# A hybrid decoder block: cross attention's scores bound behind the next projection, its turned weights in other rows, a bank for the sums of squares, and copies of the down projection's last banks

## The chip, the cores and the metric

The kernel runs on one core of a Trainium2 chip. The metric is device time in microseconds, as the median of several runs. One execution was also recorded by the hardware profiler; its span, from the first to the last instruction, is what the profile's positions refer to.

The engines are called as in the profile: PE (TensorE, matmuls; PEld is its loading of the stationary operand), DVE (VectorE), ACT (ScalarE), POOL (GpSimd) and SP (SyncE). Here POOL does almost nothing but issue DMAs, and SP nothing else.

## The reference

One decoder layer over 512 tokens of width 2048, in float32:

```
h = RMSNorm(x); one projection h @ w_in feeds
    8 sparse-attention heads (compressed, selected and window branches, gated) and
    4 gated-linear-attention heads
x = x + concat(heads) @ w_out
cq = RMSNorm(RMSNorm(x) @ w_cq, per head) / sqrt(128)       # 4 heads of 128
s  = cq . ck  over 256 memory tokens;  p = softmax(s)
x  = x + (p @ cv) @ w_co
g, u = split(RMSNorm(x) @ w_gu)                              # 2 x 5632
out = x + (silu(g) * u) @ w_down
```

All of it is computed by both versions of the kernel.

## The kernel before

**Arithmetic.** Every float32 operand of a large product is split in a high part (ACT, a cast) and a low part (DVE, the difference), both in a reduced-precision format, and a product is three matmuls: high by high, high by low, low by high (`mm3`). A weight column block costs one DMA on SP's queue into a staging buffer (tag "w", four of them, later "raw"), one cast on ACT and one subtraction on DVE, and its pair of parts lives in "wh"/"wl" (later "qh"/"ql").

**Banks.** The eight PSUM banks (512 columns each) are handed out by tag: "mm" three, "s" two, "t" two, "o" one. A tile of a tag waits until one of that tag's banks has been read for the last time by its former owner.

**Order.** The source states the order of the work, and a planner that estimates durations may let an instruction that is not ready in its estimate be passed by later ones of its engine; `high_priority(offset)` lets some (weight loads above all) go earlier. `behind(i)` makes every instruction written inside it follow `i` on `i`'s engine. Once planned, each engine runs its list strictly in that order. The side work of the projections is written as generators: `flows.tick()` is called after every six matmuls of a projection (two k tiles), and `yield n` lets n ticks pass.

**Projections and sparse-attention heads** (from about 380 to 715 us of the profile). `project` accumulates 16 k tiles into an "mm" bank: 48 matmuls. A head starts when its projection is done: it splits q, squares it, has DVE turn the squares and sum them in part (`partial_sums`), and four ticks later `total_sums` (L338) finishes the sum over the head's 128 features with one small matmul, which the profile shows as two of 16 columns ("s<-qs,every"). From the result come the factors with which ACT writes the distance biases and takes exponentials, so scores can be computed before it, but not read. Eight score blocks per head go through the two "s" banks. The first head (number 0) starts ahead of `natural(w_vsw, ...)` (L1109), a product in the other orientation that makes the values of the selected and window branches; its four accumulators take the tags "mm", "mm", "o", "mm" until `natural_end` has read them. Its side work, ticks included, runs in that product.

**Cross attention** (from about 877 to 940 us). Four heads, `cross_head` (L1198): after the head's projection, ACT and DVE split q into two Q rows; two ticks later (one in the last head) come the scores, four blocks of 128 tokens by 256 memory tokens, two per "s" bank, 12 matmuls of 256 columns; then the sums' matmul (tag "t"), the softmax on DVE and ACT in two halves "e" of 256 tokens, and the turning of the weights so that memory tokens lie on partitions. Heads 2 and 3 turn them on PE. Heads 0 and 1 turn them with DVE inside 32 x 32 blocks, write them to DRAM with POOL's DMAs and read them back in place: one tile z of tag "w" for both halves of the memory tokens, two transposes of 512 columns, four writes (one per 32 partitions, L1250), two readings into "st" rows (L1253). Ten ticks later the rows are split into "PH"/"PL" and multiplied with the values into bank "o". `spare` rows of the tags "rs" and "q1" are used only later, for squares; one of the two "q1" rows holds a piece of x.

**Down projection** (the last 480 us). It runs in four steps over 22 k-pairs, seven products in place of eight, each into a set of four banks: set 0 is "mm", "o", "t", "t", set 1 is "s", "s", "mm", "mm". After a step its banks are added to or subtracted from parts of the result ("res", `gather`). At the end of step 2 (the third) set 0 was copied by ACT into a row H (L1832), from which twelve additions were spread over step 3, one per k-pair from the fourth on (L1819); set 1 was gathered straight from its banks by eight DVE additions (`pending`, L1762) before step 3 wants them. In that step a k-pair's weights are loaded, added on DVE (L1708), cast by ACT and subtracted by DVE into "qh"/"ql" (L204).

Of the kernel before, what the change touches and what calls it, by code (L numbers as in the profile page):

```python
# [10 lines left out]
F32 = mybir.dt.float32  # L11
# [9 lines left out]
MEM = 256  # L21
# [42 lines left out]
def hybrid_block(ctx: ExitStack, tc: tile.TileContext, x_t, mem_t, sv, cmat, umask, w_a, w_r67, w_v, w_vg, w_v3,  # L64
# [14 lines left out]
    def sb(shape, tag, bufs, dt=F32):  # L79
        return (pool_b if tag in LATE else pool).tile(shape, dt, name=tag, tag=tag, bufs=bufs)  # L80
# [23 lines left out]
    def row(tag, dt=F32):  # L104
        return sb([128, 512], tag, BUFS[tag], dt)
# [89 lines left out]
    def behind(*instructions):  # L195
        stack = ExitStack()
        for i in instructions:
            stack.enter_context(tc.issue_after(i.ins))
        return stack
# [54 lines left out]
    def mm3(ps, lhs, rhs, start, stop, again=False):  # L254
        mm(ps, lhs[0], rhs[0], start=start, stop=False, skip_group_check=again)
        mm(ps, lhs[0], rhs[1], start=False, stop=False, skip_group_check=again)
        mm(ps, lhs[1], rhs[0], start=False, stop=stop, skip_group_check=again)

    def part(pair, a, n):
        return pair[0][:, a:a + n], pair[1][:, a:a + n]  # L260

    def view(t, at, *dims):
        return bass.AP(tensor=t.tensor, offset=t.offset + at, ap=[list(t.ap[0])] + [list(d) for d in dims])
# [74 lines left out]
    def total_sums(dst, part, tag):  # L338
        ps = bank(tag)
        mm(ps[:, :16], every32, part, start=True, stop=True)  # L340
        p4 = part.rearrange("p (i g) -> p i g", g=4)
        V.tensor_mul(p4, ps[:, :16].rearrange("p (i g) -> p i g", g=4),
                     own32[:, None, :].to_broadcast([128, NT, 4]))
        V.reduce_sum(dst, p4, axis=AX.X)
# [581 lines left out]
    def nsa_head(h, ps):  # L926
# [7 lines left out]
        sc, sl, neg, part_, m3 = qt[:, 0:4], qt[:, 4:8], qt[:, 8:12], qt[:, 12:28], qt[:, 28:29]  # L934
        partial_sums(part_, sq, row("n"))
        yield W_SUM + 1
        total_sums(neg, part_, "s")
        V.tensor_mul(neg, neg, rc2)
        inv_rms(sc, neg, 128, sl)
        V.tensor_mul(sc, sc, rc)  # L940
# [257 lines left out]
    def cross_head(h, ps):  # L1198
        q = row("Q", F32R), row("Q", F32R)
        sq = row("n")  # L1200
        S.activation(sq, ps, AF.Square)
        split(*q, ps, g_cq)
        cf = triple("cf")
        sc, tmp, v = cf[:, 0], cf[:, 1], cf[:, 2]
        if h < 3:
            part_ = small("qs", 2)[:, :16]
            partial_sums(part_, sq, row("n"))
        yield 1 if h == 3 else 2
        if h == 3:
            pn = bank("t")  # L1210
            for i in range(NT):
                mm(pn[:, i:i + 1], sq[:, 128 * i:128 * i + 128], one, start=True, stop=True)
        scores = [bank("s") for _ in range(2)]
        for a in range(2):
            for i in range(2):
                mm3(scores[a][:, MEM * i:MEM * i + MEM], part(q, 128 * (2 * a + i), 128), part(ckp, MEM * h, MEM),
                    start=True, stop=True)
        if h < 3:
            total_sums(v, part_, "t")
        V.tensor_mul(v, v if h < 3 else pn[:, :NT], rc[1])  # L1220
        inv_rms(sc, v, 128, tmp)
        V.tensor_mul(sc, sc, rc[0])
        sm, mn = triple("sm"), triple("mn")
        halves = []
        for a in range(2):
            s = scores[a]
            p = row("e")
            two = slice(2 * a, 2 * a + 2)
            V.tensor_reduce(mn[:, 0, two], s.rearrange("p (i n) -> p i n", i=2), axis=AX.X, op=OP.max, negate=True)
            V.tensor_mul(mn[:, 0, two], mn[:, 0, two], sc[:, two])  # L1230
            for i in range(2):
                j = 2 * a + i
                S.activation(p[:, MEM * i:MEM * i + MEM], s[:, MEM * i:MEM * i + MEM], AF.Exp,
                             bias=mn[:, 0, j:j + 1], scale=sc[:, j:j + 1], accum_out=sm[:, 0, j:j + 1])
            V.reciprocal(mn[:, 1, two], sm[:, 0, two])
            for i in range(2):
                j = 2 * a + i
                pi = p[:, MEM * i:MEM * i + MEM]
                V.tensor_scalar(pi, pi, mn[:, 1, j:j + 1], None, op0=OP.mult)
            halves.append(p)  # L1240
        rows = []
        if h < 2:
            z = sb([128, 1024], "w", 4)
            for a in range(2):
                V.transpose(view(z, 64 * a, (32, 2), (128, 8), (1, 32)), halves[a])
            d = dram.tile([128, 1024], F32, name="crossp", tag="crossp", bufs=2)
            dv = d.rearrange("(c s) (b a x) -> s b c a x", s=32, b=2, a=4)
            zv = z.rearrange("p (b c x) -> p b c x", b=2, c=4)
            for a in range(4):
                G.dma_start(dv[:, :, :, a], zv[32 * a:32 * a + 32])  # L1250
            for b in range(2):
                rows.append(row("st"))
                G.dma_start(rows[b], d[:, 512 * b:512 * b + 512])  # L1253
        yield 6 if h == 3 else 10 if h < 2 else 4
        pts = []
        for b in range(2):
            pt = sb([128, 1280], ("PH", "PL")[b], PTB, F32R)
            pts.append((pt[:, :512], pt[:, 512:1024]))
            if rows:
                split(*[view(t, 0, (32, 4), (128, 4), (1, 32)) for t in pts[b]],  # L1260
                      rows[b].rearrange("p (a i x) -> p a i x", a=4, i=NT))
                continue
            tp = bank("t")
            for i in range(NT):
                c = MEM * (i % 2) + 128 * b
                PE.transpose(tp[:, 128 * i:128 * i + 128], halves[i // 2][:, c:c + 128], ident)
            split(*pts[b], tp)
        yield 2 if h == 3 else 1
        o = bank("o")
        for b in range(2):  # L1270
            mm3(o, part(cvp[b], 128 * h, 128), pts[b], start=b == 0, stop=b == 1)
        pair = row(OC[h], F32R), row(OC[h], F32R)
        split(*pair, o)
        oc.append(pair)
# [509 lines left out]
    for step, plan in enumerate(STEPS):  # L1784
        rs_ = range(len(plan))
        for kp in range(NK):
            if step or kp % 2 == 0:
                load_w(step, kp)

            if kp == 1:  # L1790
                for s in pending:
                    gather_all(s)
                if step == 0:
                    banks[0] = banks[1]
                elif step == 2:
                    banks[1] = [bank(t) for t in SETS[1]]
                else:
                    banks = [[bank(t) for t in SETS[r]] for r in rs_]
            if kp in (1, NK - 1):
                for r in rs_ if kp == 1 else reversed(rs_):  # L1800
                    for x in range(4):
                        for k in (kp - 1, kp):
                            down_product(step, r, k, (x,))
                        if step == 3 and kp == NK - 1:
                            gather(ADD, *((0, 0), (1, 0))[r], banks[r], x, True)
            elif 1 < kp < NK - 2:
                for r in rs_:
                    down_product(step, r, kp, range(4))
            if kp in ROWS[step]:
                load_rows(*ROWS[step][kp])  # L1810
            if kp in SUMS[step]:
                add_rows(*SUMS[step][kp])
            if step == 0 and kp == 3:
                last_turn = turn(hs, NB - 1)
            if kp >= 3 or step:
                for go in last_turn.get(NK * step + kp, ()):
                    go()
            move_h(step, kp)
            if step == 3 and kp > 2 and spread:  # L1819
                with behind(*last_split):  # L1820
                    gather(*spread.pop(0))
        if step == 0:
            pending = [(COPY, 0, 1, banks[0])]
            res[0, 1] = new_res(0, 1)
        elif step == 1:
            pending = [(COPY, 0, 0, banks[0]), (COPY, 1, 1, banks[1]), (ADD, 0, 1, banks[1])]
            for a in range(2):
                res[a, a] = new_res(a, a)
        elif step == 2:
            u = quarters(sb2("H"))  # L1830
            for x in range(4):
                S.copy(u[x], banks[0][x])  # L1832
            pending = [(SUB, 1, 1, banks[1]), (ADD, 1, 0, banks[1])]
            spread = [(*p, x, last) for *p, last in ((SUB, 1, 1, u, True), (SUB, 0, 1, u, True), (ADD, 1, 0, u, False))
                      for x in range(4)]


_OUT = (4, 128, 2048)
# [120 lines left out]
```

## Time and profile before

| | |
|---|---|
| three runs, median (lowest to highest) | 2243.55 us (2241.65 to 2248.02) |
| the profiled execution | 2241.54 us |
| its span | 2239.8 us |
| PE busy | 2229.3 us, 10404 matmuls |
| DVE busy | 1709.5 us |
| ACT busy | 1159.6 us |
| POOL busy | 299.7 us |

In the timeline a row is: start, duration, engine, line of the code, operation, destination<-sources, shape, count of merged instructions, and in brackets the idle time just ahead of it with what ended it. Since almost every matmul is written in one helper (L110), they are told apart by their tiles. In the rows of windows the columns are: window, its length, then busy time and (number of instructions) of PE, PEld, DVE, ACT and POOL, the granted clock of PE, the share of DMA time and GB/s. A row of waits says who waited for whom: total, number, longest. In rows by line "a/b/c" are the shortest, median and longest in ns. Matmuls overlap, so their spacing, not their duration, is what one costs. PE counts as busy while matmuls are in its pipeline; a short wait is seen as a gap between two starts.

### The profile page before, as it was taken

Reading aid. Unit: us, or ns where it says so; the run is one execution under the profiler, and the core shown is the slowest. Engines: PE = TensorE matmul, PEld = TensorE weight load, DVE = VectorE, ACT = ScalarE, POOL = GpSimd, SP = SyncE. Lnnn points to the kernel's source line nnn. Section 1 sums busy time; section 2 is a strip of 40 time slices with the busy share of each in tenths; the row PEclk is TensorE's granted clock in tenths of the full one; section 3 lists DMA queues with packets and bytes.
Section 4 is the critical chain, followed back from the end, with each engine's and each line's share of the span. In section 5 each row is a group of like instructions: output and inputs, shape, how many; then the busy total and the mean of one; then the engine's idle time right before and its main releaser. Section 6 shows DMA issues by size and latency. Waiting matters only on the chain.

```text
span 2239.8 us, 29015 instructions
## 1 busy us (share of the span) xinstructions
PE 2229.3 (100%) x10404; PEld 1851.8 (83%) x10404; DVE 1709.5 (76%) x2653; ACT 1159.6 (52%) x1715; POOL 299.7 (13%) x453
## 2 busy tenths in 40 slices
PE   9999999999999999999999999999999999999999
PEld 8898888888887888888888888888888888888887
DVE  7648986667878336788889888988888886766786
ACT  7534564556777324575455445544554554454443
POOL 0122221122221220120011101110110011001000
PEclk9999999999999999999999999999999999999999
DMA  8588778965563983595456546554664477768684
GB/s 305 179 220 201 190 188 223 248 172 170 151 169 112 250 229 95 162 265 201 148 184 197 173 150 195 189 170 154 198 201 142 150 281 261 268 241 281 250 278 163
DMA packets 130784, 448.23 MB, mean 200 GB/s; under 512 B 16240, under 2 KB 17520, under 8 KB 127696
## 3 DMA queue, kind: packets, MB, share of 16 engines
q1 hardware_dynamic: 81040, 304.71, 39.8%
q0 software_dynamic: 47152, 137.39, 24.7%
q10 hardware_dynamic: 2448, 4.28, 0.5%
q8 instruction: 81, 1.33, 0.2%
q14 instruction: 63, 0.52, 0.1%
HBM read 401.10 MB, written 107.09 MB: 227 GB/s over the span
## 4 chain that ended last, share of the span: by engine, by line
PE 96%; DVE 2%; DMA 1%; ACT 1%; issue 1%; SPq 0%; DVEq 0%; POOLq 0%; ACTq 0%
PE mm L110 52%; PE t L110 18%; PE s L110 14%; PE o L110 11%; PE t L1072 1%; DMA raw<-gu 0%; DMA raw<-td 0%; DMA PH<-w_ck 0%; DMA ss<-q 0%; DMA ss<-KV 0%; DVE ql L204 0%; DVE e L741 0%; DVE P L1017 0%; DVE wl L204 0%; ACT wh L204 0%
## 5 line engine op out<-in xcount | busy, mean ns | idle before, releaser
L204 ACT CAST qh<-raw 128x1024 fp32r<-128x1024 f32 (+1 forms) x494 | 478.5, 976 | 468.2 <-PE o L110 128.0
L204 DVE TENSOR_TENSOR ql<-raw,qh 128x1024 fp32r<-128x1024 f32 (+1 forms) x494 | 550.6, 1124 | 106.1 <-PE mm L110 40.1
L110 PE MATMUL mm<-X,wh 128*128 128x512 f32 x1664 | 524.4, 394 | 0.0
L110 PEld LDWEIGHTS mm<-X,wh 128*128 128x128 f32 x1664 | 306.4, 188 | 59.1 <-issue 0.8
L110 PE MATMUL t<-qh,PB 128*128 128x512 f32 x968 | 333.0, 389 | 0.0
L110 PE MATMUL mm<-X,wl 128*128 128x512 f32 x832 | 325.6, 392 | 0.5 <-DVE wl L204 0.5
L110 PE MATMUL mm<-qh,PB 128*128 128x512 f32 x868 | 309.1, 389 | 0.1
L204 DVE TENSOR_TENSOR wl<-w,wh 128x1024 fp32r<-128x1024 f32 (+2 forms) x172 | 205.5, 1200 | 130.8 <-ACT wh L204 127.9
L204 ACT CAST wh<-w 128x1024 fp32r<-128x1024 f32 (+2 forms) x172 | 176.8, 1033 | 232.9 <-PE mm L110 151.8
L110 PE MATMUL s<-qh,PB 128*128 128x512 f32 x672 | 231.0, 389 | 0.0
L110 PE MATMUL mm<-qh,PA 128*128 128x512 f32 x640 | 220.0, 389 | 0.0
L110 PEld LDWEIGHTS t<-qh,PB 128*128 128x128 f32 x968 | 181.7, 188 | 37.9
L110 PEld LDWEIGHTS mm<-qh,PB 128*128 128x128 f32 x868 | 163.0, 188 | 34.2 <-ACT qh L204 0.7
L110 PE MATMUL t<-ql,PB 128*128 128x512 f32 x484 | 188.3, 389 | 0.0
L110 PE MATMUL o<-qh,PB 128*128 128x512 f32 x484 | 187.4, 389 | 0.0
L110 PEld LDWEIGHTS mm<-X,wl 128*128 128x128 f32 x832 | 156.2, 188 | 33.9 <-DVE wl L204 1.8
L110 PE MATMUL mm<-ql,PB 128*128 128x512 f32 x434 | 169.3, 390 | 1.1 <-DVE ql L204 1.1
L110 PEld LDWEIGHTS s<-qh,PB 128*128 128x128 f32 x672 | 126.1, 188 | 25.9
L110 PEld LDWEIGHTS mm<-qh,PA 128*128 128x128 f32 x640 | 120.1, 188 | 25.0
L110 PE MATMUL s<-ql,PB 128*128 128x512 f32 x336 | 131.0, 390 | 0.1
L110 PE MATMUL mm<-ql,PA 128*128 128x512 f32 x320 | 124.5, 389 | 0.0
L1424 DVE TENSOR_TENSOR raw<-raw 128x1024 f32<-128x1024 f32 x80 | 97.0, 1223 | 18.8 <-DMA raw<-w_gu 18.4
(534 smaller groups left out, 3493.4 us busy)
## 6 DMA issues: line engine op xcount, KB each, us to landing
raw<-w_gu SPq DMA_DIRECT2D x80, 768.0 KB, 4.2
raw<-w_down SPq DMA_DIRECT2D x88, 512.0 KB, 4.8
raw<-w_gu SPq DMA_DIRECT2D x80, 512.0 KB, 3.6
td<-w_down POOLq DMA_DIRECT2D x66, 512.0 KB, 7.4
w<-w_a SPq DMA_DIRECT2D x60, 512.0 KB, 6.3
raw<-td SPq DMA_DIRECT2D x22, 1024.0 KB, 6.7
w<-w_out SPq DMA_DIRECT2D x32, 512.0 KB, 6.1
HR<-h POOLq DMA_DIRECT2D x28, 512.0 KB, 4.5
```

Of the source, the lines that this page charges most:

```text
L110: last_mm[0] = PE.matmul(*args, **kw)
L204: last_split[:] = S.copy(hi, src), V.tensor_sub(lo, src, hi)
L1072: PE.transpose(tp[:, 128 * (i - j):128 * (i - j) + 128], ps_[b][:, POFF[i] + 128 * j:POFF[i] + 128 * j + 128], ident)
L1424: V.tensor_add(raw[:, 0:1024], raw[:, 0:1024], raw[:, 512:1536])
```

## The change

- The squares' sums of a sparse-attention head take a bank of the tag "mm" instead of "s".
- Cross attention's scores are bound behind the last matmul written before them.
- In cross attention's heads 0 and 1, z becomes two rows, of the tags "q1" and "rs", one for each half of the memory tokens; each half has two transposes of 256 columns, four writes to a DRAM tile of its own, and its reading.
- At the end of step 2 of the down projection, set 1 is copied by ACT too, into four "PA" rows; all 20 additions are spread over step 3, one per k-pair, from the second k-pair on.

```
-        total_sums(neg, part_, "s")
+        total_sums(neg, part_, "mm")
...
         scores = [bank("s") for _ in range(2)]
-        for a in range(2):
-            for i in range(2):
-                mm3(scores[a][:, MEM * i:MEM * i + MEM], part(q, 128 * (2 * a + i), 128), part(ckp, MEM * h, MEM),
-                    start=True, stop=True)
+        with behind(last_mm[0]):
+            for a in range(2):
+                for i in range(2):
+                    mm3(scores[a][:, MEM * i:MEM * i + MEM], part(q, 128 * (2 * a + i), 128), part(ckp, MEM * h, MEM),
+                        start=True, stop=True)
...
         if h < 2:
-            z = sb([128, 1024], "w", 4)
-            for a in range(2):
-                V.transpose(view(z, 64 * a, (32, 2), (128, 8), (1, 32)), halves[a])
-            d = dram.tile([128, 1024], F32, name="crossp", tag="crossp", bufs=2)
-            dv = d.rearrange("(c s) (b a x) -> s b c a x", s=32, b=2, a=4)
-            zv = z.rearrange("p (b c x) -> p b c x", b=2, c=4)
-            for a in range(4):
-                G.dma_start(dv[:, :, :, a], zv[32 * a:32 * a + 32])
             for b in range(2):
-                rows.append(row("st"))
-                G.dma_start(rows[b], d[:, 512 * b:512 * b + 512])
+                z = row(("q1", "rs")[b])
+                for a in range(2):
+                    V.transpose(view(z, 64 * a, (32, 2), (128, 4), (1, 32)),
+                                view(halves[a], 128 * b, (MEM, 2), (1, 128)))
+                d = dram.tile([128, 512], F32, name="crossp", tag="crossp", bufs=6)
+                for a in range(4):
+                    G.dma_start(d[:, 128 * a:128 * a + 128].rearrange("(c s) x -> s c x", s=32),
+                                z[32 * a:32 * a + 32].rearrange("s (c x) -> s c x", c=4))
+                rows.append(d)
+            for b in range(2):
+                t = row("st")
+                G.dma_start(t, rows[b])
+                rows[b] = t
...
-            if step == 3 and kp > 2 and spread:
+            if step == 3 and kp and spread:
                 with behind(*last_split):
                     gather(*spread.pop(0))
...
-            pending = [(SUB, 1, 1, banks[1]), (ADD, 1, 0, banks[1])]
-            spread = [(*p, x, last) for *p, last in ((SUB, 1, 1, u, True), (SUB, 0, 1, u, True), (ADD, 1, 0, u, False))
-                      for x in range(4)]
+            w = [sb2("PA") for _ in range(4)]
+            for x in range(4):
+                S.copy(w[x], banks[1][x])
+            pending = []
+            spread = [(*p, x, last) for *p, last in ((SUB, 1, 1, w, False), (ADD, 1, 0, w, False), (SUB, 1, 1, u, True),
+                                                     (SUB, 0, 1, u, True), (ADD, 1, 0, u, False)) for x in range(4)]
```

## The prediction

> **What bounds the kernel now.** I read the profile from the whole to the single wait: the page's busy times, the chain that ended last, TensorE's waits, then the timeline at each place that the diff touches.
>
> ```profile
> span 2239.8 us, 29015 instructions
> PE 2229.3 (100%) x10404; PEld 1851.8 (83%) x10404; DVE 1709.5 (76%) x2653; ACT 1159.6 (52%) x1715; POOL 299.7 (13%) x453
> ...
> PE 96%; DVE 2%; DMA 1%; ACT 1%; issue 1%; SPq 0%; DVEq 0%; POOLq 0%; ACTq 0%
> ```
>
> ```profile
> 1000.00:1100.00 100.00, 100.00 (x443) 82.61 (x442) 83.77 (x106) 53.18 (x63) 5.09 (x8) 1.00 0.56 192
> ```
>
> TensorE is the bound, 96% of the chain. In an undisturbed stretch 443 matmuls of 512 columns take 100 us, so one leaves every 0.226 us. The change removes no matmul, so all it can win is time in which the next matmul comes later than that. The waits of TensorE in the whole run are nine groups, of which the first and the last are
>
> ```profile
> PE mm L110 <- DVE ql L204: 1.1, 2, 0.9
> ...
> PE o L110 <- DVE e L1058: 0.2, 1, 0.2
> ```
>
> so at most 9 x 1.1 = 9.9 us stand there. 0.3% of the time before is 6.7 us, about what a measurement of this kernel can tell from no change. No single edit reaches it.
>
> **The sums' bank.** Between 505 and 660 us the weight loads (they run ahead of the matmuls and wait first) have this row, and the timeline shows one of its five cases:
>
> ```profile
> PEld s L110 <- PE o L110: 1.7, 5, 0.4
> ```
>
> ```profile
> 542.99 0.55 DVE L1017 CUSTOM_DVE_ANT_0 P<-s,P 128x384 f32<-128x384 f32 x1
> 543.18 0.27 PE L110 MATMUL o<-PH,KV 128*128 128x128 f32 x1
> 543.66 0.30 PEld L110 LDWEIGHTS s<-qs,every 128*128 128x128 f32 x2 [0.36 <-PE o L110]
> 543.70 0.37 PE L110 MATMUL s<-qs,every 128*128 128x16 f32 x2 [0.25 <-DVE mn L1017]
> ```
>
> The two tiny matmuls that sum a head's squares want one of two "s" banks; both hold scores, and the bank comes free when VectorE has read it (542.99 + 0.55 = 543.54). The page names "PE o", but that product was long issued; the reader of "s" came last. The "mm" tag has three banks, of which the running projection holds one, and the previous one was read out by then. I take the five waits as gone: **-1.7**. The next scores, at 544.6, want the bank freed at 543.5, so coming 0.4 us sooner they still find it free.
>
> The first head differs. Its sums come in the middle of the product for the values of the selected and window branches, whose four accumulators hold all three "mm" banks (and "o") until it ends:
>
> ```profile
> 388.69 0.29 PE L110 MATMUL s<-qs,every 128*128 128x16 f32 x2
> ...
> 439.02 0.61 PE L110 MATMUL mm<-X,wh 128*128 128x512 f32 x2
> ```
>
> ```profile
> 435.98 1.43 DVE L207 SCALAR_TENSOR_TENSOR KV<-mm,rc,KV 128x512 fp32r<-128x512 f32 x2 [1.81 <-ACT KV L206]
> ```
>
> 439.02 is the next projection's start; the first accumulator is read out half way through the two reads at 435.98, at 436.7. So this head's sums move from 388.7 to about 437, 48 us later, and behind them all that needs its norm: the biases, the exponentials and the release of its score banks and Q rows, which ran between 391 and 413.3 us. TensorE's order lets other matmuls past, so what counts is whether the other engines can hold the moved work:
>
> ```profile
> 391.00:413.30 22.30, 22.30 (x124) 19.29 (x123) 15.67 (x58) 14.79 (x30) 3.50 (x5) 1.00 0.82 211
> 437.00:460.00 23.00, 22.97 (x117) 18.20 (x116) 15.31 (x22) 9.97 (x16) 2.86 (x4) 1.00 0.79 241
> ```
>
> ```profile
> L204 DVE TENSOR_TENSOR wl<-w,wh 128x1024 fp32r<-128x1024 f32 x7 | 8.5, 1224 | 1.5 <-ACT wh L204 1.5
> ```
>
> (the last row from the groups of 388 to 414 us.) Without the splitting of weights, which stays where it is, the head costs VectorE some 15.7 - 8.5 = 7.2 us; 437 to 460 would then hold 15.3 + 7.2 = 22.5 of 23. That is full, but TensorE has cover: the next two projections are 2 x 48 matmuls, 21.7 us, and a third bank holds another 10.8. I expect small waits only, where scores meet a busy VectorE: between 0 and 8 x 0.5 = 4 us (eight score blocks, each at most the longest wait above, rounded up), and take **+0.7**, near the lower end, since the rows of the other heads show 0.4 or less at one block in eight.
>
> **Cross attention.** The source puts a head's scores two ticks (12 matmuls) into the next projection. In the second head two of the twelve were ordered ahead of those matmuls:
>
> ```profile
> 894.14 0.61 PE L110 MATMUL mm<-X,wh 128*128 128x512 f32 x2
> 894.84 0.68 ACT L206 ACTIVATE Q<-mm,vecs 128x512 fp32r<-128x512 f32 x1
> 895.57 0.51 PE L110 MATMUL s<-P,Q 128*128 128x256 f32 x2 [0.81 <-ACT Q L206]
> ```
>
> The third matmul was due at 894.14 + 2 x 0.226 = 894.59 and came at 895.57, a loss of 1.0 us. Bound behind the projection's last matmul all twelve come 2.7 us after the projection, at 897.1; VectorE's half of Q, the later one, is done at about 896.2. **-1.0.** The other three heads are in that place already.
>
> What is late next is the product with the values, which waits for rows that went through DRAM:
>
> ```profile
> PEld o L110 <- ACT PH L204: 1.4, 4, 0.5
> ```
>
> ```profile
> 893.56 2.54 POOL L1250 DMA_DIRECT2D crossp<-w  x4 [39.49 <-DVE w L1245]
> 899.72 1.11 POOL L1253 DMA_DIRECT2D st<-crossp  x2 [3.63 <-DMA crossp<-w]
> ```
>
> ```profile
> L508 POOL DMA_DIRECT2D ck<-Q x8: 549/550/566, 64.4 to 68.3; - x8
> ...
> crossp<-w POOLq DMA_DIRECT2D x8, 128.0 KB, 3.7
> ck<-Q POOLq DMA_DIRECT2D x8, 64.0 KB, 3.5
> ```
>
> The product is already late by up to 0.5 us, and TensorE gets there 1 us sooner. In the first two heads GpSimd now issues eight writes of 64 KB for four of 128 KB. The kernel has such writes for the keys (ck): 0.55 us each on GpSimd, 3.5 us to land. Eight take 4.4 us against 2.5. But each half's reading waits for its own four only: if the first write leaves at 893.6, the first half can be read at 893.6 + 4 x 0.55 + 3.5 = 899.3 (now 899.7), the second at 901.5 (now 900.3). Nothing else waits on GpSimd's queue there. Of the 1.0 us between 0 and all is given back here; I take 0.3, since the first half comes no later: **+0.3**.
>
> The Trainium skill speaks against this edit (DMA: Bandwidth & Descriptors, section Bandwidth): batch transfers, for those under 64 KB are dominated by their descriptors. These are 64 KB, at its edge. By its formula (Anatomy of one DMA) of about 2.0 us plus bytes over 436e3, an estimate for eight is 17.2 us against 9.2 for four if they ran one after another, so 8 us more per head. The trace does not agree that they do: four left within 2.54 us and the reader behind them started 3.6 us after the last.
>
> The transposes become four of 256 columns for two of 512:
>
> ```profile
> L1245 DVE STREAM_TRANSPOSE w<-e x4: 703/711/714, 891.1 to 906.7; 128x512 f32<-128x512 f32 x4
> ```
>
> ```profile
> L973 DVE STREAM_TRANSPOSE pcz<-pc 128x128 f32<-128x128 f32 x1 | 0.3, 304 | 0.0
> ```
>
> Between 304 ns for 128 columns and 711 for 512, some 440 each: 4 x 0.44 - 2 x 0.71 = 0.34 us more on VectorE, well inside the 12 us until the product, so 0. The staging buffer that z no longer takes can only let a weight load start sooner, and no weight load is late there: 0 too.
>
> **The down projection after step three.** Eight additions out of banks leave VectorE at the step's end for four copies on ScalarE; the additions follow from the copies, one per k-pair.
>
> ```profile
> 2111.47 0.58 ACT L1832 COPY H<-mm 128x512 f32<-128x512 f32 x1
> 2114.01 2.00 ACT L204 CAST qh<-raw 128x1024 fp32r<-128x1024 f32 x2
> 2114.19 1.28 DVE L1762 TENSOR_TENSOR T<-T,mm 128x512 f32<-128x512 f32 x2
> 2115.38 2.36 DVE L204 TENSOR_TENSOR ql<-raw,qh 128x1024 fp32r<-128x1024 f32 x2
> 2115.40 0.39 PE L110 MATMUL o<-qh,PB 128*128 128x512 f32 x1
> 2116.66 0.50 PE L110 MATMUL mm<-ql,PB 128*128 128x512 f32 x1 [0.87 <-DVE ql L204]
> ```
>
> A matmul due at 2115.63 came at 2116.66, 1.0 us late, after the low half of a weight that VectorE could begin only behind two additions. Without them it still needs the high half, which ScalarE has at 2114.01 + 2.00/2 = 2115.0. So the split starts 0.3 us sooner, not 1.3, and unless TensorE's order changes only that is won. The same crossing one step earlier shows the other order:
>
> ```profile
> 1996.04 0.62 PE L110 MATMUL o<-qh,PB 128*128 128x512 f32 x2
> 1996.50 0.49 PE L110 MATMUL mm<-ql,PB 128*128 128x512 f32 x1
> ```
>
> There the "o" products stand ahead of the same matmul, and no wait is shown at it. So between -0.3 and -1.0; I take **-0.3**, as nothing in the diff asks for the other order. The copies, 4 x 0.58 = 2.3 us, are ready from the second half's last matmuls, some 5 us ahead of the casts. The additions keep their number and now begin with the second k-pair instead of the fourth:
>
> ```profile
> 2120.00:2240.00 120.00, 115.79 (x510) 95.23 (x508) 89.53 (x87) 48.01 (x46) 4.25 (x8) 0.99 0.63 220
> ```
>
> VectorE is 75% busy there (89.53 of 120) and the last addition ends a k-pair before the end: 0.
>
> **The sum.** -1.7 + 0.7 - 1.0 + 0.3 - 0.3 = -2.0 us. Against the profiled execution, which took 2241.5 us (1.7 us around the span), that is 2239.5. The three runs have their median at 2243.55, 2.0 us above it, and begin at 2241.65, 0.1 above it. Three runs don't tell which of the two is the typical time, so I add half of the 2.0 and forecast a median of **2240.5 us**: no change that can be measured.
>
> **The rivals.**
>
> The waits only move. The evidence for it is above: behind each wait stands a second late thing (the cast, the rows from DRAM, a busy VectorE). Then the -3.0 gross comes back whole and the time stays at 2241.5 to 2243.5. Against it speaks only the sums' bank, whose next user has its bank in time. Chance 0.25.
>
> Slower: the first head's moved work does not fit. It decides where scores and exponentials of that head last longer than TensorE's cover. They began 2.3 us after the sums (391.0 less 388.7) and took 22.3 us; 2.3 us after 437 and at that pace they end at 461.6, and the cover (two projections and a third bank, 32.5 us from 439.0) ends at 471.5. At less than 0.7 of the pace the Q rows are still held when the third bank is full, and TensorE stands. VectorE at 22.5 of 23 us speaks for it, its 12.5 us of load in the next 20 against:
>
> ```profile
> 460.00:480.00 20.00, 20.00 (x108) 17.16 (x107) 12.50 (x45) 12.28 (x28) 2.26 (x3) 1.00 0.63 136
> ```
>
> At half the pace they end at 439.3 + 44.6 = 483.9, 12.4 us beyond the cover: 2240.5 + 12.4 = 2253. Chance 0.08.
>
> Slower by transfers that follow one another: if a 64 KB write held GpSimd's queue for its 3.5 us, eight would take 28.0 us and four of 3.7 us 14.8, so the products of two heads would come 13.2 us later each, at worst 2240.5 + 26 = 2267. The 2.54 us for four writes speak against it. Chance 0.02. The Trainium skill's rule on batching (DMA: Bandwidth & Descriptors, Bandwidth) would lead this way.
>
> The edits do more than their waits: TensorE takes the other order at the down projection, no wait comes back, and the first head costs nothing: -1.7 - 1.0 - 1.0 = -3.7, so 2238.8. Chance 0.10. For more than 6.7 us the order of the whole head stage would have to improve; the nine groups of waits leave little for it: 0.05.
>
> A part that does not do what it says: the binding finds no later matmul to stand behind and the two scores stay first. That costs the forecast its 0.7 and leaves 2241.2, inside the forecast's own range.
>
> **How the numbers follow.** The forecast has the remaining 0.50. It, the moved waits and the -3.7 case lie within 0.3% (2236.8 to 2250.3): 0.50 + 0.25 + 0.10 = 0.85. Faster by more 0.05; slower by more 0.08 + 0.02 = 0.10. The unknown costs reach from -3.7 (2238.8) to +2.3 (the first head at 4.0 instead of 0.7, all of the 1.0 given back instead of 0.3, nothing won at the down projection), 2244.8; the runs before lay 1.9 below to 4.5 above their median, of which a median keeps some half. I take **2236.5 to 2247**, which leaves out the slower cases and most of the faster.
>
> **What would show it.** Right: no wait of the sums' matmuls between 505 and 660 us; the first head's sums at about 437 and its scores after them; all twelve scores of cross attention's second head together, 12 matmuls behind the projection; a product with "st" rows that waits up to 0.5 us longer; the wait on "ql" at the down projection's step smaller but there. Wrong: any single idle stretch of TensorE over 1 us between 437 and 510, or GpSimd's writes more than 0.7 us apart. A time outside 2236.8 to 2250.3 would mean that the order of a whole stage has changed, which I do not foresee.

## The result and the profile after

The changed kernel takes **2264.28 us** (six runs, 2263.02 to 2271.74) beside 2242.46 us of the kernel before in the same rounds: a ratio of **1.0098 [1.0081, 1.0114]**, slower by some 22 us. The forecast was 2240.5 us, with a range of 2236.5 to 2247.

The page of the profile after (its execution took 2271.74 us, the longest of the six):

```profile
span 2269.9 us, 29048 instructions
PE 2238.3 (99%) x10404; PEld 1858.2 (82%) x10404; DVE 1709.9 (75%) x2657; ACT 1161.7 (51%) x1719; POOL 303.5 (13%) x461
```

No engine got much more work: ScalarE is busy 2.1 us longer than before, GpSimd 3.8, VectorE 0.4. The matmuls are the same 10404. The rows of windows say where the time stands (columns as before: PE, PEld, DVE, ACT, POOL, granted clock):

```profile
391.00:413.30 22.30, 22.30 (x110) 18.48 (x109) 9.85 (x13) 6.71 (x10) 4.28 (x5) 1.00 0.83 200
437.00:460.00 23.00, 11.12 (x40) 8.71 (x40) 14.20 (x65) 13.24 (x32) 1.61 (x3) 0.74 0.34 107
```

Between 437 and 460 us TensorE is busy for 11.12 us of 23, where it was busy for 22.97, and VectorE, which was expected full there, for 14.20. From 391 to 413 VectorE has 5.8 us less, the first head's work (7.2 was the estimate). The list of TensorE's waits now begins with four groups that were small or absent; before, no single wait was above 0.9 us:

```profile
PE t L110 <- ACT Q L204: 8.6, 1, 8.6
PE s L110 <- DVE mn L1017: 6.5, 2, 6.3
PE s L110 <- DVE e L741: 4.4, 3, 3.8
PE mm L110 <- ACT wh L204: 2.3, 2, 1.1
```

A measure for the comparisons below: for each pair of neighbouring matmuls, the distance of their starts less the median distance for that width (its columns), summed by stretch ("excess"). Over the whole run it is 24.7 us before and 54.8 after, a difference of 30.1 for 30.1 us of span. Of it 26.5 lie between 400 and 500 us (1.7 before, 28.2 after). The third group above is a gap at 186 us, in a stage that the change doesn't touch; it comes back at the end.

TensorE's timeline of the place:

```profile
441.50 0.31 PE L110 MATMUL mm<-qs,every 128*128 128x16 f32 x2
...
448.44 2.06 PE L110 MATMUL s<-KS,Q 128*128 128x416 f32 x6 [6.31 <-DVE mn L1017]
450.73 3.98 PE L110 MATMUL s<-KV,Q 128*128 128x128 f32 x12 [0.23 <-DVE mn L1017]
463.33 0.47 PE L110 MATMUL t<-wl,Q 128*64 128x256 f32 x1 [8.62 <-ACT Q L204]
...
471.95 0.63 PE L110 MATMUL mm<-X,wh 128*128 128x512 f32 x2
```

The first head's sums did move to the end of the values' product (441.50). But the next projection, the cover that the prediction counted on, starts only at 471.95. In its place TensorE waits twice, for the head's banks and then for "t<-wl,Q": these are the third and fourth of the four units by which the values are compressed (`compress_unit`), 16 matmuls each. Before, they ran inside the product, the fourth at its end:

```profile
424.16 0.28 PE L110 MATMUL t<-wl,Q 128*64 128x256 f32 x1
...
437.10 0.28 PE L110 MATMUL t<-wl,Q 128*64 128x256 f32 x1
```

Why they are late stands in GpSimd's timeline, first before, then after:

```profile
408.10 0.61 POOL L113 DMA_DIRECT2D pcd<-pcz  x1
414.60 1.66 POOL L113 DMA_DIRECT2D e<-pcd  x3 [5.88 <-ACT wh L204]
...
416.98 1.04 POOL L817 MEMSET e<- 128x512 f32 x1
420.55 0.54 POOL L817 MEMSET e<- 128x512 f32 x1 [2.52 <-DVE Q L204]
```

```profile
456.94 0.60 POOL L113 DMA_DIRECT2D pcd<-pcz  x1 [17.86 <-DVE pcz L973]
459.52 1.66 POOL L113 DMA_DIRECT2D e<-pcd  x3 [1.98 <-DMA pcd<-pcz]
461.17 0.54 POOL L817 MEMSET e<- 128x512 f32 x1
464.19 0.52 POOL L817 MEMSET e<- 128x512 f32 x1 [2.48 <-DVE Q L204]
```

A head sends its weights over the compressed positions through DRAM and gets them back in a row of the tag "e" (`load_blocks`); the units' blocks of input are cleared in rows of the same tag (L817), two rows in all. In both kernels the clearing of the third and fourth block follows the first head's row. That row hangs on the head's norm, hence on the sums. It comes 45 us later, the blocks with it, and the units behind them.

And why the projection could not go ahead of them is in ACT's casts of weights:

```profile
442.17 1.04 ACT L204 CAST wh<-w 128x1024 fp32r<-128x1024 f32 x1 [0.24 <-PE mm L110]
465.95 1.03 ACT L204 CAST wh<-w 128x1024 fp32r<-128x1024 f32 x1
467.50 1.04 ACT L204 CAST wh<-w 128x1024 fp32r<-128x1024 f32 x1
470.53 1.04 ACT L204 CAST wh<-w 128x1024 fp32r<-128x1024 f32 x1 [1.99 <-PE t L110]
```

"wh" has three buffers. The units need four blocks of weights, eight matmuls to a block, and each cast after 442.17 comes as eight unit matmuls end: three of the four blocks sat in the three buffers until the units ran. The cast at 465.95 is the units' fourth block, and the projection's first is the one at 467.50.

### The profile page after: what moved, and what is told of

Same layout as the page of the kernel before. It is cut to its first block, busy times and chain, and to the rows that moved or that the text cites. A ratio compares the mean times of both kernels' runs of the same rounds, so it can differ in the third digit from the quotient of the medians.

```text
span 2269.9 us, 29048 instructions
## 1 busy us (share of the span) xinstructions
PE 2238.3 (99%) x10404; PEld 1858.2 (82%) x10404; DVE 1709.9 (75%) x2657; ACT 1161.7 (51%) x1719; POOL 303.5 (13%) x461
## 4 chain that ended last, share of the span: by engine, by line
PE 95%; DVE 2%; DMA 1%; ACT 1%; issue 1%; POOL 0%; SPq 0%; DVEq 0%; POOLq 0%; ACTq 0%
PE mm L110 51%; PE t L110 18%; PE s L110 14%; PE o L110 11%; PE t L1072 1%; DMA KV<-Q 0%; DVE wl L204 0%; ACT wh L204 0%; DMA raw<-td 0%; DMA raw<-gu 0%; DMA PH<-w_ck 0%; DVE ql L204 0%; DVE e L741 0%; DVE P L1017 0%; DVE KV L676 0%
```

## The experiments

Each kernel was timed beside the kernel before (2243.8 to 2244.3 us there). Two changes of one line first part the suspects.

**e1: the kernel before, with the first head's sums alone in "mm".**

```
-        total_sums(neg, part_, "s")
+        total_sums(neg, part_, "s" if h else "mm")
```

> The kernel before, with one edit: the first head alone takes its sums' bank from the tag mm. Theory A (this one move makes the whole loss: the sums wait for an accumulator of the running product, and all that hangs on them comes 50 us late): 2242.5 us plus the 26.5 us by which TensorE's gaps between 400 and 500 us grew, so 2264 to 2270, with the sums at about 435 to 442 us and gaps of TensorE of 20 us or more behind them. Rival C (the loss lies in the other heads' sharing of the mm banks or in the other edits): within 3 us of 2242.5.

Measured: 2268.88 us, ratio 1.0114 [1.0098, 1.013]; excess from 400 to 500 us 28.0. The two waits are there at the same length (together 15.6 us of excess; gaps of 20 us or more were expected):

```profile
441.94 2.06 PE L110 MATMUL s<-KS,Q 128*128 128x416 f32 x6 [6.31 <-DVE mn L1017]
...
456.82 0.48 PE L110 MATMUL t<-wl,Q 128*64 128x256 f32 x1 [8.61 <-ACT Q L204]
```

So the whole loss is the move of one head's two small matmuls.

**e2: the change, with all sums back in "s".**

```
-        total_sums(neg, part_, "mm")
+        total_sums(neg, part_, "s")
```

> The changed kernel with every head's sums back in the tag s, so cross attention's and the down projection's edits alone. Theory A: 2242.5 less 1.1 (cross attention's wait) less 0.3 (down projection) = 2241.1, within 1.5 us. Rival C (these edits carry part of the loss): 2245 or more. In the profile the five waits of the sums between 505 and 660 us are back, 0.4 us each.

Measured: 2242.01 us, ratio 0.9992 [0.9982, 1.0001]. The other three edits cost nothing that can be measured, and the sums' five waits are back in the weight loads:

```profile
PEld s L110 <- PE o L110: 1.7, 5, 0.4
```

**e3: the change, with the first head's sums alone in "s".**

```
-        total_sums(neg, part_, "mm")
+        total_sums(neg, part_, "mm" if h else "s")
```

> The changed kernel with the first head's sums alone back in the tag s; the other seven stay in mm. Theory A: 2242.5 less 1.9 (the five sums' waits) less 1.1 less 0.3 = 2239.2, within 1.5 us; TensorE's gaps beyond the usual spacing between 400 and 700 us sum to about 6 us (8 before, 30 after the change). Rival C (sharing the mm banks costs in the other heads): above 2245, with gaps at the starts of projections.

Measured: 2240.42 us, ratio 0.9981 [0.9972, 0.9989]: faster than both kernels. Excess from 500 to 700 us falls from 6.3 (before) to 3.5.

**e4: the change, with the first head's returned weights in a row of another tag.** The sums of all heads stay in "mm".

```
         def load_blocks():
-            t = row("e")[:96]
+            t = row("e" if h else "M")[:96]
```

> The changed kernel, but the row into which a head's compressed weights come back from DRAM is taken from the tag M in the first head and not from e. Theory A1 (rows of a tag are handed out in the order in which they are asked for; the values' third and fourth compression blocks ask for e behind the first head's late row, and their waiting units hold the weight buffers and TensorE's list): the blocks' clearing on GpSimd comes before 430 us and not at 461, the 9 us gap before the units at 463 is gone and the two gaps of 1.3 us at 427 and 434 too; what is left is the wait for the scores behind the sums, at most 7 us: 2244 to 2252. Rival B (the units wait for Q rows that the first head's scores hold, or the scores alone stop TensorE): the units stay behind the scores and the time stays within 4 us of 2264.

Measured: 2238.79 us, ratio 0.9979 [0.997, 0.9988], better than expected: neither the head's banks nor the units wait. GpSimd clears the two blocks 74 and 63 us sooner than after the change, far ahead of the head's row; the units and the projection follow their old places, and the head's scores go in between the projection's matmuls:

```profile
387.57 0.98 POOL L817 MEMSET e<- 128x512 f32 x1
...
400.93 1.00 POOL L817 MEMSET e<- 128x512 f32 x1
...
455.93 1.82 POOL L113 DMA_DIRECT2D M<-pcd  x3 [2.50 <-DMA pcd<-pcz]
```

```profile
433.36 0.31 PE L110 MATMUL mm<-qs,every 128*128 128x16 f32 x2
...
435.71 0.62 PE L110 MATMUL mm<-X,wh 128*128 128x512 f32 x2
...
446.01 1.11 PE L110 MATMUL s<-KS,Q 128*128 128x416 f32 x6
```

```profile
437.00:460.00 23.00, 22.97 (x113) 17.92 (x112) 21.05 (x76) 15.46 (x38) 4.45 (x7) 1.00 0.68 196
```

The sums stand at the end of the values' product as in the changed kernel, 45 us later than before, and the loss is gone. It was the shared tag. VectorE carries 21.05 of 23 us and TensorE doesn't stop.

**e5: the values' units load their weights without priority.** Two gaps of 1.3 us (at 427 and 434 us, "PE mm <- ACT wh" above) stand in the product itself. The guess was that units' weights, cast early, leave the product one buffer.

```
-        w = Weights(w_c1[which, lu], 2048)
+        w = Weights(w_c1[which, lu], 2048, ahead=0 if which else 400)
```

> The changed kernel, but the weights of the values' compression units are split when the unit is written, not some 400 instructions ahead. Theory A2 (the waiting units' split weights hold two of the three wh buffers from 415 us on, so that the running product works from one buffer): the two gaps of 1.3 us at 427 and 434 us are gone, and the time falls by about 2.6 us to 2261.5. If the freed buffers also let the next projection start ahead of the units, it falls by up to 20 us. Rival (the two gaps come from late loads of weights): both gaps stay and the time stays at 2264 within 1.5 us.

Measured: 2265.89 us, ratio 1.0091 [1.0076, 1.0107]; both gaps stay at 1.3. But the casts did not move either (ACT has them at 414.71, three in a row, then 422.17, 427.61 and 434.83; after the change 414.58, 422.03, 427.47, 434.70), so the run doesn't test the guess. For it speaks that three casts stand in a row where the product takes one per 5.4 us, and that each later one starts as the block before it has had its last matmul. Both gaps are absent in e4. It is argued, not shown.

**e8 and e9: a third "e" row; the clearing on VectorE.** What does a late row hold up: two rows too few, GpSimd's queue (its transfer waits 17.86 us for "pcz" with the clearing behind it), or the order of the requests?

```
-    BUFS = {..., "st": 6, "e": 2, ...}
+    BUFS = {..., "st": 5, "e": 3, ...}
```

> The changed kernel, all heads' sums in "mm", with three rows for the tag "e" in place of two (and five "st" rows for six, to make room). Theory of the order (rows of a tag are granted in the order in which the source asks for them, and the first head's row is asked for before the rows of the values' third and fourth compression blocks, so those stand behind it however many rows there are): the two blocks are still cleared behind the reading of the first head's row, near 460 us, the gaps of 6.6 and 9 us stay, 2262 to 2269 us. Theory of the count (two rows are too few: the head's row and one block hold both): at least the third unit goes back to its place near 424 us, the longer gap shrinks by 5 us or more, below 2258 us.

```
-        G.memset(blk, 0.0)
+        V.memset(blk, 0.0)
```

> The changed kernel with the compression blocks cleared by VectorE instead of GpSimd, so that they no longer stand in GpSimd's queue behind the first head's transfer, which waits for VectorE there. Theory of GpSimd's queue (the blocks are late only because GpSimd executes in order and its transfer waits): the third block at least is filled before 430 us, and the time comes to 2240 to 2252 us. Theory of the row order: the clearing still follows the first head's work, now on VectorE, gaps of 6.6 and 9 us stay within 1 us each, 2262 to 2270 us.

Measured: e8 2264.01 us, ratio 1.0083 [1.007, 1.0096], gaps of 6.6 and 9.0; e9 2262.83 us, ratio 1.0081 [1.0066, 1.0095], gaps of 6.6 and 7.0. With three rows both blocks are cleared in one go, still right behind the head's row:

```profile
453.77 1.66 POOL L113 DMA_DIRECT2D e<-pcd  x3 [1.97 <-DMA pcd<-pcz]
455.42 1.01 POOL L817 MEMSET e<- 128x512 f32 x2
```

In e9 the first clearing stands on VectorE in the midst of the head's last work (L998):

```profile
454.56 0.48 DVE L817 MEMSET e<- 128x512 f32 x1
454.95 0.30 DVE L998 TENSOR_SCALAR P<-P,cf 128x384 f32<-128x384 f32 x1
```

The order holds in both. GpSimd's queue is worth 2 us (9.0 against 7.0), more than the 1 us that was allowed for but far from the loss; the third row is worth nothing. Each of the two runs leaves the other suspect in place, but e4 answers for both: there, with two rows, GpSimd's list has the clearing ahead of the same head's transfers as soon as these use another tag, so its queue didn't force the order. What binds is that rows of a tag are given out in the order in which the source asks for them, and the head, whose code starts ahead of the product, asks first.

**e6: e3 with the old turning of cross attention's weights** (one tile z, four writes of 128 KB).

> The changed kernel with the first head's sums in s, and with the turning of cross attention's weights as it was before (one z in a staging buffer, two transposes, four writes per head). Theory of the prediction, as it failed (the product with the values would come to wait once TensorE is 1 us earlier, and the new rows keep it from that): the weight load of the first head's product waits 0.5 to 1.3 us for its rows, and the time is 0 to 1 us above the run with the new rows, 2239.2 to 2240.5. Rival (the rows come early enough either way, since the planned place of the product follows the rows): no wait over 0.3 us, 2239.2.

Measured: 2242.29 us, ratio 0.9986 [0.9976, 0.9995]. The product with the "st" rows now waits longer (an excess of 0.39 us; 0.22 before), and so does the sums' matmul behind the scores (0.38):

```profile
905.96 0.50 PE L110 MATMUL o<-PH,st 128*128 128x512 f32 x1 [0.23 <-ACT PH L204]
```

The times of e3 and e6 overlap; the waits tell them apart, in one profile each. No profile with the new rows waits at that product, except that of e8 (0.6 us in two places), which has one "st" row fewer.

**e7: e3 with the first k-pair of the down projection's last step ordered two banks at a time**, so that the first product with "ql" comes later.

```
                     for x in range(4):
+                        if step == 3 and kp == 1:
+                            if x % 2 == 0:
+                                for k in (0, 1):
+                                    down_product(step, r, k, (x, x + 1))
+                            continue
                         for k in (kp - 1, kp):
```

> The changed kernel with the first head's sums in s, and in the down projection's step 3 the first two k-pairs are multiplied into two banks at a time: the first k-pair into both, then the second into both. So six matmuls of the first k-pair, not three, stand ahead of the first that needs the second k-pair's weights. Theory (the wait that is left there is the cast and subtraction of that weight, 0.7 us late): the gap of 0.7 us at the step falls to 0.15 or less and the time to 2239.2 less 0.6 = 2238.6. Rival (the buffers of the weight come free only with the last matmul of step 2, and the list changes elsewhere): a gap of 0.5 us or more stays, one k-pair later.

Measured: 2238.8 us, ratio 0.9978 [0.9967, 0.9988]. The gap at the step is gone (excess from 2100 to 2200 us -0.15; 0.37 in e3). But it is gone in the profiles of e4, e5 and e9 too, which have the old order, so it is not shown that the order removed it.

**e10: e4 and e7 together.**

> The changed kernel with the two mends that gained: the first head's row of compressed weights taken from the tag "M" instead of "e" (so that all sums can stay in "mm"), and, in step three of the down projection, the products of the first k-pair ordered two banks at a time. The first gave a ratio of 0.9979 alone, the second took some 0.4 us of wait at one matmul. If they add: 2238.0 to 2239.0 us against 2243.8 before, a ratio of 0.9974 to 0.9980; no gap over 0.3 us in the sparse-attention heads nor behind the third step. If the wait of the down projection only moves to the next pair of banks: as with the first alone, 2238.8 or above.

Measured: 2240.07 us, ratio 0.9979 [0.9971, 0.9988]. The two don't add by anything that five rounds can tell; e3, e4, e7 and e10 are equal within their intervals, all some 0.2% faster than the kernel before.

## Why the prediction was wrong, point by point

**The step that failed** is the price of the first head's move: "TensorE's order lets other matmuls past, so what counts is whether the other engines can hold the moved work", with "TensorE has cover: the next two projections". The term was +0.7 and measured +26.5. The move was placed right (at the end of the values' product, 53 us later where 48 was foretold), and the bearing of the other engines too: where only they count, in e4, VectorE carries 21.05 us (22.5 foretold) and the excess from 400 to 500 us is 2.5 against 1.7 before, +0.8. But the moved work's products were listed only as banks and Q rows. It also asks for an "e" row, ahead of the values' compression blocks; these feed units which stand in TensorE's list ahead of the projection and whose weights hold all three "wh" buffers that the projection needs. The cover was behind the thing that it should cover. The trace of before had it: GpSimd's "e<-pcd" at 414.60 with the clearing right behind it, and a second clearing that waits for a row.

The 26.5 us by parts, as excess: the two waits 6.6 + 9.0, the two gaps of 1.3, together 18.2. The units' 32 matmuls then last from 463.33 to 471.95, 8.6 us, at a spacing twice that of e4 (0.21 to 0.12 us):

```profile
464.17 0.41 PE L110 MATMUL t<-wl,Q 128*64 128x256 f32 x1
464.39 0.42 PE L110 MATMUL t<-wh,Q 128*128 128x256 f32 x1
```

```profile
463.30:467.00 3.70, 3.67 (x16) 3.39 (x16) 2.58 (x5) 1.92 (x4) 0.52 (x1) 0.50 0.00 0
```

At e4's spacing they take 32 x 0.12 = 3.8, so 4.8 more: 1.2 of it is a wait of the fourth unit for its Q row (at 467.35), the other 3.6 the wider spacing. The remaining 3.5 are the scores between the waits (2.06 us for six against 1.11) and smaller ones. The doubled spacing is the granted clock: 0.50 in the row above and from 448.4 to 454.7, 1.00 again from 472 on. A wait of TensorE costs more than its length here. The Trainium skill (TensorE: Matmul & The Clock Gate, Part 1) has the clock fall to half after an idle window of about 3.4 us; the trace agrees, with 6.3 and 8.6 us idle and twice the spacing behind them. That the length alone does not decide it is seen in the last section.

**The sums' bank:** right in kind, too small in size. Taking the sums of heads 1 to 7 out of "s" was worth 2.8 us of excess between 500 and 700 us (6.3 before, 3.5 in e3) where 1.7 was foretold.

**Cross attention:** -1.0 and +0.3 foretold. All twelve scores come together, without a wait, 2.7 us after the projection's start (924.16):

```profile
926.88 1.73 PE L110 MATMUL s<-P,Q 128*128 128x256 f32 x12
...
935.28 0.43 PE L110 MATMUL o<-PH,st 128*128 128x512 f32 x1
```

The -1.0 is there, and nothing is given back: the product with "st" has no wait. With the old rows (e6) it waits 0.4 in the one profile, so the fear was right for the binding alone, and the split rows mend it. The eight writes take 4.45 us, 0.55 each, as foretold (4.4), and the first reading leaves right behind them, the second 3.2 us later:

```profile
923.88 2.27 POOL L1251 DMA_DIRECT2D crossp<-q  x4 [39.93 <-DVE q L1247]
926.13 2.18 POOL L1251 DMA_DIRECT2D crossp<-rs  x4
928.29 0.58 POOL L1256 DMA_DIRECT2D st<-crossp  x1
931.46 0.56 POOL L1256 DMA_DIRECT2D st<-crossp  x1 [2.59 <-ACT cf L304]
```

The rival in which the transfers follow one another is out.

**The down projection:** -0.3 foretold, and in this one profile found: the excess before the "ql" product is 0.74 for 1.03. That was luck. With the same edit and the same order of TensorE it is 0.5 in e2, 0.4 in e3, 0.2 in e6 and e8, and nothing in e4, e5 and e9; without the edit it is 1.03 twice (before and e1). First after, then e4:

```profile
2143.05 1.23 DVE L1712 TENSOR_TENSOR raw<-raw 128x1024 f32<-128x1024 f32 x1 [1.65 <-DMA raw<-td]
...
2145.33 2.35 DVE L204 TENSOR_TENSOR ql<-raw,qh 128x1024 fp32r<-128x1024 f32 x2
2145.42 0.61 PE L110 MATMUL mm<-qh,PB 128*128 128x512 f32 x2
2146.61 0.50 PE L110 MATMUL mm<-ql,PB 128*128 128x512 f32 x1 [0.57 <-DVE ql L204]
```

```profile
2109.64 1.22 DVE L1712 TENSOR_TENSOR raw<-raw 128x1024 f32<-128x1024 f32 x1 [0.91 <-DMA raw<-td]
...
2111.82 2.01 ACT L204 CAST qh<-raw 128x1024 fp32r<-128x1024 f32 x2
2111.92 2.35 DVE L204 TENSOR_TENSOR ql<-raw,qh 128x1024 fp32r<-128x1024 f32 x2
2113.20 0.50 PE L110 MATMUL mm<-ql,PB 128*128 128x512 f32 x1
```

The prediction let the subtraction wait for the cast that starts just ahead of it (2115.0 there). In e4 it starts 0.1 us after that cast begins, so it reads an earlier one, and the limit of 0.3 doesn't hold. In both it starts 2.28 us after VectorE's addition of the weight (L1712), with one other subtraction between, and that addition waits for the transfer "raw<-td". Before, the two additions out of banks came on top: without them the subtraction of 2115.38 would have started at 2114.19, early enough. So the edit takes away all of the 1.0, and what is left is as late as the transfer lands.

**The slower rival** ("the first head's moved work does not fit", 0.08) had the place and the sign, not the mechanism: its limit at 471.5 us was never reached by the head's scores, which are done by 455, and VectorE was idle for 8.8 of the 23 us instead of overfull. The sign that was named for it, an idle stretch of TensorE of over 1 us between 437 and 510, came twice. The chances were wrong too: of the 0.10 for slower, the 0.08 for this head rested on one mechanism, though a move of some 50 us of a head's work passes many requests for rows.

Without the first head the prediction's own terms give -1.7 - 1.0 + 0.3 - 0.3 = -2.7 us; e3, which is that, measured 2240.42 beside 2243.79, -3.4. The sum is near, but made of terms that were off: the sums' bank gave more, and the down projection varies.

## What to carry to other kernels

When a step moves later, list every tile that the work behind it asks for, not only the banks that it frees, and look up who asks for the next tile of the same tag: where rows are given out in the order of the source, one late owner holds up all who ask after it, and here a third row did not help. Before work is counted as cover, check that it can start: its weights, buffers and place in the engine's list must not stand behind the thing that waits. If such a move is wanted, give the late owner a tag of its own; here one word in one line turned +22 us into -5. Leaving the first head's sums where they were (e3) is as good within the intervals.

## What the runs showed of the hardware that was not expected

A gap at 186 us (scores that wait for VectorE's "e", L741, in the earlier stage) differs from profile to profile: none in e1 and e4, 0.3 us before, 0.4 in e8, 1.5 in e2 and e7, 1.8 in e9, 2.4 in e6, 3.1 to 4.0 in e3, e10, e5 and after. It hangs on a transfer: ahead of it VectorE waits for "KV<-Q" from GpSimd's queue, 0.73 us in e1, 1.86 in e4, 4.38 before, and 7.17, 7.62, 8.02 and 8.09 in e3, e10, e5 and after. That, and not the change, may be a part of the 7.5 us by which the profiled execution of the changed kernel lies above its median; the other five were not profiled. Why the transfer lands late was not tried.

What follows the gap was not expected either. After 3.8 us of idle time (after, e5) the next matmuls of 512 columns are 0.43 us apart instead of 0.23, and so they are after 2.3 us in e6, where the granted clock is 0.50 from 190 to 192 us. After 2.9 us in e3 and 3.4 in e10 they are not, and the clock is 1.00. So the length of one wait does not tell whether the clock falls; what does was not tried.
